# Output projection in five unequal groups of chunks, residual scaled in place

## The chip, the cores and the metric

The kernel runs on one core of a Trainium2 chip. The metric is device time in microseconds of one execution, median over runs. The engines have one instruction queue each and run it in order: TensorE (PE in the profile, its weight loads PEld), VectorE (DVE), ScalarE (ACT), GpSimd (POOL) and SyncE (SP), which here only issues transfers.

## The reference, cut to what matters

One layer on 1024 tokens and 16 meta tokens, width 1024. A normalised input is projected; three mixers (pooling, 256 columns; forgetting attention and stick-breaking attention, 384 columns each) give y of 1024 columns. Then:

```python
h = h + jnp.concatenate([y_pool, y_fox, y_sb], axis=-1) @ w_out[i]
a = rmsnorm(h, norm2[i])
h = h + (jax.nn.silu(a @ w_gate[i]) * (a @ w_up[i])) @ w_down[i]
```

and a final norm. The change concerns the first of these lines and the scaling in the second.

## The kernel before

**Precision.** Every fp32 operand is split into a high part and the rest. A product of two such operands takes three matmuls: high by high, high by rest, rest by high. The split of y and of the weights `w_out` is done on POOL: a copy (`hi_pool`, which the profile gives as L77) and a subtraction (L681 or L674 for weights, L690 for y).

**Output projection.** y lies in eight chunks of 128 columns in memory (`ysd`), and `w_out` in eight chunks of 128 rows. The residual `h` (tile `x1`, in the profile x) has eight token blocks of 128 x 1024, blocks 0 to 3 are half j = 0, blocks 4 to 7 are j = 1. The chunks are summed in four groups of two, `OGROUPS = ((5, 2), (3, 4), (0, 1), (6, 7))`, each for both halves, so in eight passes. `out_load` prepares a pass: weights of the group, if they aren't there, and the y chunks of the half. `out_part` walks its four token blocks, `out_block` does one: for each half of the 1024 columns, 2 x 3 matmuls into one PSUM tile `mm` (two buffers), and an addition of it into `h` on VectorE (L703). That is 8 passes x 4 blocks x 2 = 64 additions.

**Buffers.** Weights of groups 0 and 2 use the four `xa` tiles, those of groups 1 and 3 the four `wa` tiles, two per chunk. A y chunk takes two of eight `xb` tiles; raw data pass through `yr` (three) and `wor` (two). A tile is taken again as soon as its last reader is done.

**What runs beside it.** The attention of six pairs of heads is one stream, everything else (input projections, then the output projection) another, the filler. `interleave` mixes their emission by estimated costs: `GOALS` says how much filler goes beside each pair, `X5` how much beside the last, whose chunk 7 is the last y to come. A scheduler then orders each engine's queue by priority; attention gets a boost of 300. The last pair walks its tiles from large to small (t = 3 to 0, both heads of each), and its `head_norm` makes `last_y[1]` (tiles 3 and 2) and `last_y[0]` (tiles 1 and 0). Its sum passes ScalarE, POOL (tile `pt`; ScalarE for the last), VectorE and two matmuls with `hmean` (L410, L411), then L413 to L415 and the split (L566, L567).

**The last passes.** Group 3, chunks 6 and 7, is done by `out_last`, j = 1 and then j = 0. After a block's additions it squares `h` on ScalarE into a scratch tile `hs` (an `xa` tile), makes the norm's factor `r2`, writes `hs = h * r2`, and stores `h` to memory (`hsd`, SP), where the end of the kernel fetches it. `turn_block` transposes `hs` on PE, `split_block` splits it into `bs`.

**Behind it.** The gated network starts with two chunks done directly (`direct`, L890, chunk pairs with the j = 1 half first, then j = 0), then ten rounds of a Strassen scheme (`strassen`), whose first weight loads stand in SP's queue behind stores of the direct part.

Of the kernel before, what the change touches and what calls it, by code (L numbers as in the profile page):

```python
# [8 lines left out]
F32 = mybir.dt.float32  # L9
F32R = mybir.dt.float32r  # L10
BF16 = mybir.dt.bfloat16
AF = mybir.ActivationFunctionType
# [3 lines left out]
D = 1024  # L16
# [14 lines left out]
def hymba_trunk(  # L31
# [19 lines left out]
    nc = tc.nc  # L51
    V, S, G, PE = nc.vector, nc.scalar, nc.gpsimd, nc.tensor

    def pool(name, side=None, space=None, bufs=1):
        kw = {}
        if side is not None:
            kw["side"] = side
        if space is not None:
            kw["space"] = space
        return tc.tile_pool(name=name, bufs=bufs, reuse_waits="tile", **kw)  # L60
# [3 lines left out]
    def T(p, shape, dt, tag, bufs=1):  # L64
        uid[0] += 1
        return p.tile(list(shape), dt, tag=tag, bufs=bufs, name=f"{tag}_{uid[0]}")
# [3 lines left out]
    PAIRS = [((i >= 3), (2 + i - 3 if i >= 3 else 11 + i), 2 * (i % 3), (2 + i - 3 if i >= 3 else 5 + i))  # L70
             for i in (0, 3, 4, 5, 1, 2)]
# [4 lines left out]
    def hi_pool(o, i):  # L76
        G.tensor_scalar(o, i, 1.0, 0.0, ALU.mult, ALU.add)  # L77
# [9 lines left out]
    x0 = x0_stack.enter_context(pool("x0", side="right"))  # L87
# [3 lines left out]
    def mm(tag, shape, bufs):  # L91
        return T(ps, shape, F32, tag, bufs)
# [272 lines left out]
    def project(pr, c):  # L365
        WPE[0] = G
        w = wload(c + 3)
        new_keys(pr)
        for t0, n in KPIECES:
            o = []  # L370
            yield from proj_piece(w, t0, n, o)
            keys(pr, t0, n, o[0])
        w = wload(c)
        new_queries(pr)
        for j in (1, 0):
            o = []
            yield from proj_piece(w, NM + 512 * j, 512, o)
            queries(pr, j, o[0])
        yield from values(pr, c + 6)
# [283 lines left out]
    def split_weights(g, c):  # L663

        wp, tag = (x0, "xa") if g % 2 == 0 else (regions["wo"], "wa")
        wh = T(wp, [128, D + 32 * (g % 2 == 0)], F32R, tag, 4)[:, :D]
        wl = T(wp, [128, D + 32 * (g % 2 == 0)], F32R, tag, 4)[:, :D]
        if g == 0:
            for q in range(4):
                raw = T(r1, [128, 2, 128], F32, "wr", 4).rearrange("p a b -> p (a b)")  # L670
                qs = slice(256 * q, 256 * q + 256)
                nc.sync.dma_start(raw, w_out[128 * c:128 * c + 128, qs])
                hi_pool(wh[:, qs], raw)
                G.tensor_tensor(wl[:, qs], raw, wh[:, qs], ALU.subtract)  # L674
        else:
            for q in range(2):
                raw = T(regions["wo"], [128, 512], F32, "wor", 2)
                qs = slice(512 * q, 512 * q + 512)
                nc.sync.dma_start(raw, w_out[128 * c:128 * c + 128, qs])
                hi_pool(wh[:, qs], raw)  # L680
                G.tensor_tensor(wl[:, qs], raw, wh[:, qs], ALU.subtract)  # L681
        return wh, wl

    def split_y(c, j):
        raw = T(x0, [128, T0], F32, "xb", 8)[:, :512] if regions["wo"] is None else T(regions["wo"], [128, 512], F32, "yr", 3)
        nc.sync.dma_start(raw, ysd[c][:, 512 * j:512 * j + 512])
        yh = T(x0, [128, T0], F32R, "xb", 8)[:, :512]
        hi_pool(yh, raw)
        yl = T(x0, [128, T0], F32R, "xb", 8)[:, :512]
        G.tensor_tensor(yl, raw, yh, ALU.subtract)  # L690
        return yh, yl

    def out_block(b, tb, yy, ws):
        ts_ = slice(128 * tb, 128 * tb + 128)
        for dh in range(2):
            ds = slice(512 * dh, 512 * dh + 512)
            p = mm("mm", [128, 512], MMB)
            i = 0
            for (yh, yl), (wh, wl) in zip(yy, ws):
                for y_, w_ in ((yh, wh), (yh, wl), (yl, wh)):  # L700
                    PE.matmul(p, y_[:, ts_], w_[:, ds], start=i == 0, stop=i == 3 * len(ws) - 1)  # L701
                    i += 1
            V.tensor_tensor(h[b][:, ds], p, h[b][:, ds], ALU.add)  # L703
            yield 0.65 * len(ws)

    def out_load(g, j):
        if g not in wts:
            wts[g] = [split_weights(g, c) for c in OGROUPS[g]]
        return [last_y[j] if c == PAIRS[5][3] else split_y(c, j) for c in OGROUPS[g]]

    def out_part(g, j, yy=None):

        if yy is None:
            yy = out_load(g, j)
        for tb in range(4):
            yield from out_block(4 * j + tb, tb, yy, wts[g])

    def out_last(j):

        step = out_part(len(OGROUPS) - 1, j, ylast[j])  # L720
        for tb in range(4):
            b = 4 * j + tb
            next(step)
            next(step)
            hs = T(x0, [128, D + 32], F32, "xa", 4)[:, :D]
            S.activation(hs, h[b], AF.Square, accum_out=ssq2[:, b:b + 1])
            if j:
                S.activation(r2[:, b:b + 1], ssq2[:, b:b + 1], AF.Ln, scale=1.0 / D, bias=epst[:, 0:1])
                S.activation(r2[:, b:b + 1], r2[:, b:b + 1], AF.Exp, scale=-0.5)
            else:  # L730
                G.tensor_scalar(r2[:, b:b + 1], ssq2[:, b:b + 1], 1.0 / D, EPS, ALU.mult, ALU.add)
                G.tensor_tensor(r2[:, b:b + 1], r2[:, b:b + 1], mhalf[:, 0:1], ALU.pow)
            S.activation(hs, h[b], AF.Copy, scale=r2[:, b:b + 1])
            nc.sync.dma_start(hsd[b], h[b])
            hss[b] = hs
            yield 1.3

    def turn_block(b):
# [16 lines left out]
    OGROUPS = ((5, 2), (3, 4), (0, 1), (6, 7))  # L755
    wts, bf, bs, hss, last_y = {}, {}, {}, {}, {}
    dpool = ctx.enter_context(tc.tile_pool(name="dp", bufs=1, space=bass.MemoryType.DRAM))
    ysd = {c: dpool.tile([128, SEQ], F32, name=f"ysd{c}") for c in range(8)}
    hsd = [dpool.tile([128, D], F32, name=f"hsd{b}") for b in range(8)]
# [4 lines left out]
    ssq2 = cst.tile([128, 8], F32, name="ssq2")  # L764
    r2 = cst.tile([128, 8], F32, name="r2")
# [37 lines left out]
    def after(g, n, s):  # L803

        for i, c in enumerate(g):
            yield c
            if i == n:
                yield from s

    regions = {"wo": None}  # L810
    h = {}

    def open_out():
        first = out_load(0, 1)
        for b in (4, 5, 6, 7, 0, 1, 2, 3):
            h[b] = T(hp, [128, D], F32, "x1", 8)
            nc.sync.dma_start(h[b], xtok[NM + 128 * b:NM + 128 * b + 128, :])
        r1_stack.close()
        wos.enter_context(x0_stack.pop_all())
        regions["wo"] = wos.enter_context(pool("wo", side="right"))  # L820
        yield from out_part(0, 1, first)

    wos = ExitStack()
    project_first(prs[0], PAIRS[0][1])
# [5 lines left out]
    def filler():  # L830
        for p in range(1, 6):
            gen = project(prs[p], PAIRS[p][1])
            if p == 1:
                gen = after(gen, FGS, forget_gates())
            for ci in range(2):
                if p == POOLS[ci]:
                    yield from pool_pieces(ci)
            yield from gen
        yield from open_out()
        for g, j in ((0, 0), (1, 1), (1, 0), (2, 1), (2, 0)):  # L840
            yield from out_part(g, j)

    SBC, FOXC = 65.0, 38.0
    PC, UC = 32.6, 12.0
    AHEAD, X4, X5, X6 = 12.0, 20.0, 43.0, 12.0
    BOOST = 300
    POOLS = (2, 4)
    GOALS = (PC + 8, PC + 4, PC, PC + UC, PC - AHEAD + X4, X5)
    att, f = Stream(attention(), BOOST), Stream(filler())
    goal = AHEAD  # L850
    for p in range(6):
        goal += GOALS[p]
        interleave(att, FOXC if PAIRS[p][0] else SBC * (0.7 if p == 5 else 1), f, goal - f.at)
    f.finish()
    g = len(OGROUPS) - 1
    ylast = {1: out_load(g, 1)}
    y6 = split_y(OGROUPS[g][0], 0)
    f = Stream(out_last(1))
    interleave(att, SBC * 0.3, f, X6)
    f.finish()  # L860
    ylast[0] = [y6, last_y[0]]
    at_stack.close()
    attn_stack.close()

# [41 lines left out]
    for _ in out_last(0):  # L906
        pass
# [105 lines left out]
    for c0 in range(2, FF, 2):  # L1013
# [6 lines left out]
        for key, x in up.items():  # L1020
            g = gate[key]
# [34 lines left out]
    h = {}  # L1056
# [123 lines left out]
```

## Time and profile before

| what | value |
|---|---|
| three runs, median | 1284.89 us (1284.74 to 1286.3) |
| profiled execution | 1286.02 us, span 1284.2 us |
| granted TensorE clock, mean | 0.982 |
| PE busy, share of span | 1215.3 us, 95% |
| DVE busy | 947.2 us, 74% |
| ACT busy | 630.5 us, 49% |
| POOL busy | 480.2 us, 37% |
| L701, first and last start | 474.8 and 633.9 us |
| L703, 64 additions, median | 681 ns |

The span is from the first to the last instruction; the 1.8 us beside it lie around them. Matmuls are pipelined, so that a row of several has a duration longer than the distance of their starts; a pace is read from the starts. In rows of a timeline the columns are start, duration, engine, line, operation, output and inputs, shapes, count, and in brackets the engine's idle time before it and who ended it.

### The profile page before, as it was taken

What the parts mean: (1) busy time and instruction counts of PE and PEld (TensorE: products, weight loads), DVE (VectorE), ACT (ScalarE), POOL (GpSimd) and SP (SyncE); (2) the same over time, 40 slices, a digit from 0 to 9 for tenths busy, and PEclk for the clock granted to TensorE, in tenths of its full rate; (3) what the DMA queues carried; (4) which work ended last, traced back from release to release, by engine and by line L of the source; (5) the groups of instructions that cost most, each with busy time, mean ns of one, the idle gap of its engine ahead of it and who ended that gap; (6) DMA issues with size and microseconds to landing.
All of it is one profiled execution on the core that took longest, in us unless ns stands there. A gap on an engine that the chain in (4) does not pass through costs nothing.

```text
span 1284.2 us, 18471 instructions
## 1 busy us (share of the span) xinstructions
PE 1215.3 (95%) x6310; PEld 1023.5 (80%) x6310; DVE 947.2 (74%) x1713; ACT 630.5 (49%) x1318; POOL 480.2 (37%) x534
## 2 busy tenths in 40 slices
PE   7699899999898989999898999999999999999997
PEld 5587778888788878778687888888888888788885
DVE  8667886868977779997777676666767656876557
ACT  6456754645448677767743333332223334444443
POOL 6459046362363764550105453443544410000001
PEclk9999899999899989999999999999999999999999
DMA  5100011010100161201505554445544439565653
GB/s 180 40 17 27 13 47 34 26 42 18 50 29 30 38 213 67 74 25 50 197 25 180 171 167 151 138 136 181 189 164 160 136 131 344 172 212 199 197 173 139
DMA packets 73146, 147.13 MB, mean 115 GB/s; under 512 B 9052, under 2 KB 21340, under 8 KB 73052
## 3 DMA queue, kind: packets, MB, share of 16 engines
q1 hardware_dynamic: 69728, 142.01, 33.3%
q10 hardware_dynamic: 3324, 3.95, 0.9%
q8 instruction: 50, 0.82, 0.3%
q14 instruction: 44, 0.36, 0.1%
HBM read 103.98 MB, written 41.94 MB: 114 GB/s over the span
## 4 chain that ended last, share of the span: by engine, by line
PE 66%; DVE 11%; issue 4%; ACT 4%; DMA 2%; POOL 1%; SPq 0%; DVEq 0%; POOLq 0%; ACTq 0%
PE s L890 21%; PE mm L289 10%; PE mm L890 8%; PE s L1075 7%; PE mm L701 4%; PE o L511 4%; PE mm L1075 3%; PE o L1075 3%; PE s L531 3%; DVE r L470 3%; PE s L429 1%; PE s L431 1%; DVE x L703 1%; DVE P L472 1%; DMA raw<-in_w_down 1%
## 5 line engine op out<-in xcount | busy, mean ns | idle before, releaser
L890 PE MATMUL s<-t,wh 128*128 128x512 f32 x544 | 170.4, 392 | 3.5 <-ACT wh L876 3.5
L890 PEld LDWEIGHTS s<-t,wh 128*128 128x128 f32 x544 | 102.7, 189 | 25.7 <-ACT wh L876 4.2
L890 PE MATMUL s<-s,wh 128*128 128x512 f32 x384 | 118.5, 390 | 0.0
L876 ACT CAST wh<-ss 128x512 fp32r<-128x512 f32 x80 | 49.5, 621 | 133.6 <-PE s L890 93.0
L890 PE MATMUL s<-t,wl 128*128 128x512 f32 x272 | 106.3, 391 | 0.0
L289 PE MATMUL mm<-x,wh 128*128 128x512 f32 (+1 forms) x320 | 100.1, 387 | 1.1 <-DVE pt L354 1.1
L538 ACT CAST ph<-s 128x512 fp32r<-128x512 f32 (+2 forms) x168 | 70.7, 434 | 60.0 <-PE s L531 23.9
L890 PE MATMUL mm<-t,wh 128*128 128x512 f32 x320 | 98.5, 389 | 0.0
L1063 ACT CAST wh<-sg 128x512 fp32r<-128x512 f32 x74 | 46.0, 623 | 104.6 <-PE s L1075 46.1
L876 ACT CAST wh<-raw 128x512 fp32r<-128x512 f32 x68 | 41.7, 621 | 111.2 <-PE s L890 72.4
L539 DVE TENSOR_TENSOR pl<-s,ph 128x512 fp32r<-128x512 f32 (+2 forms) x168 | 81.1, 492 | 19.9 <-ACT ph L538 17.5
L1064 DVE TENSOR_TENSOR wl<-sg,wh 128x512 fp32r<-128x512 f32 x74 | 51.0, 690 | 56.9 <-ACT wh L1063 56.6
L511 PE MATMUL o<-pl,v 128*128 128x256 f32 (+1 forms) x288 | 85.8, 314 | 0.7 <-DVE pl L521 0.6
L511 PE MATMUL o<-ph,v 128*128 128x256 f32 (+1 forms) x288 | 80.2, 292 | 3.8 <-ACT ph L520 2.4
L890 PEld LDWEIGHTS s<-s,wh 128*128 128x128 f32 x384 | 71.9, 188 | 14.9
L984 DVE TENSOR_TENSOR cg<-s,tmp 128x512 f32<-128x512 f32 x60 | 41.2, 687 | 56.9 <-PE s L890 56.9
L1114 POOL TENSOR_TENSOR r<-r,mhalf 128x1 f32<-128x1 f32 x8 | 4.4, 547 | 209.0 <-DVE r L1113 207.4
L289 PE MATMUL mm<-xa,wh 128*128 128x264 f32 (+3 forms) x248 | 78.5, 320 | 1.2 <-ACT rbc L239 0.7
L289 PE MATMUL mm<-xa,wl 128*128 128x264 f32 (+3 forms) x248 | 76.5, 313 | 1.2 <-POOL wl L164 1.2
L289 PE MATMUL mm<-xb,wh 128*128 128x264 f32 (+3 forms) x248 | 77.0, 313 | 0.0
L531 PE MATMUL s<-ident,P 128*128 128x128 f32 x432 | 68.8, 278 | 6.3 <-DVE pl L521 3.6
L878 DVE TENSOR_TENSOR wl<-ss,wh 128x512 fp32r<-128x512 f32 x80 | 68.7, 862 | 8.2 <-ACT wh L876 6.8
(287 smaller groups left out, 3636.6 us busy)
## 6 DMA issues: line engine op xcount, KB each, us to landing
sg<-lsd SPq DMA_DIRECT2D x70, 256.0 KB, 3.2
raw<-in_w_gate SPq DMA_DIRECT2D x22, 512.0 KB, 5.4
raw<-in_w_up SPq DMA_DIRECT2D x22, 512.0 KB, 3.9
wr<-in_w_in SPq DMA_DIRECT2D x80, 128.0 KB, 2.2
raw<-in_w_down SPq DMA_DIRECT2D x20, 512.0 KB, 3.6
lsd<-cg SPq DMA_DIRECT2D x40, 256.0 KB, 3.2
raw<-rsd SPq DMA_DIRECT2D x40, 256.0 KB, 3.4
raw<-in_w_down SPq DMA_DIRECT2D x34, 256.0 KB, 3.1
```

Source lines behind the costliest of these rows:

```text
L289: PE.matmul(p[:, :n], w[k][ww], xx(k, t0, n), start=i == 0, stop=i == 23)
L511: PE.matmul(po[:, c:256], pr.v[h][:, kb, :], x, start=first and ix == 0, stop=(kb == nkb - 1 and ix == 1), skip_group_check=True)
L531: PE.transpose(tp[:, gi, ii, :], ptiles[ii][:, kc], ident)
L538: S.copy(ph[:, a:b], tpf[:, a:b])
L539: V.tensor_tensor(pl[:, a:b], tpf[:, a:b], ph[:, a:b], ALU.subtract)
L701: PE.matmul(p, y_[:, ts_], w_[:, ds], start=i == 0, stop=i == 3 * len(ws) - 1)
L876: S.copy(wh, a)
L878: V.tensor_tensor(wl, a, wh, ALU.subtract)
L890: PE.matmul(p, ws[ww][:, k, :], xs_[xx][:, k, :], start=first and i == 0, stop=i == 11, skip_group_check=True)
L1063: S.copy(wh, a)
L1064: V.tensor_tensor(wl, a, wh, ALU.subtract)
L1075: PE.matmul(p, x[xx][:, 128 * b:128 * b + 128], y[yy], start=first and i == 0, stop=last and i == 2, skip_group_check=True)
```

## The change

The chunks are summed in five passes: group 0 for j = 1; groups 0 and 1 for j = 0; groups 1 and 2 for j = 1; group 3 for j = 1; groups 2 and 3 for j = 0. A pass of two groups sums 4 x 3 matmuls in one PSUM tile, so there are 5 x 4 x 2 = 40 additions; the matmuls are the same 384. The weights of groups 2 and 3, four chunks, are resident in `xa` and `wa` during the last pass. The y chunks of that pass are prepared ahead of the j = 1 pass of group 3. As `xa` is then taken, `h` is scaled in place; the square's result goes, in bf16, into a `wor` tile, and the store of `h` stands ahead of the square, since the scaling overwrites what it reads. `X5` goes from 43 to 32.

```diff
-    def out_load(g, j):
-        if g not in wts:
-            wts[g] = [split_weights(g, c) for c in OGROUPS[g]]
-        return [last_y[j] if c == PAIRS[5][3] else split_y(c, j) for c in OGROUPS[g]]
+    def out_load(gs, j):
+
+        for g in gs:
+            if g not in wts:
+                wts[g] = [split_weights(g, c) for c in OGROUPS[g]]
+        return [last_y[j] if c == PAIRS[5][3] else split_y(c, j) for g in gs for c in OGROUPS[g]]
...
-            yield from out_block(4 * j + tb, tb, yy, wts[g])
+            yield from out_block(4 * j + tb, tb, yy, [w for g in gs for w in wts[g]])
...
-            hs = T(x0, [128, D + 32], F32, "xa", 4)[:, :D]
-            S.activation(hs, h[b], AF.Square, accum_out=ssq2[:, b:b + 1])
+            nc.sync.dma_start(hsd[b], h[b])
+            sq = T(regions["wo"], [128, D], BF16, "wor", 2)
+            S.activation(sq, h[b], AF.Square, accum_out=ssq2[:, b:b + 1])
...
-            S.activation(hs, h[b], AF.Copy, scale=r2[:, b:b + 1])
-            nc.sync.dma_start(hsd[b], h[b])
-            hss[b] = hs
+            S.activation(h[b], h[b], AF.Copy, scale=r2[:, b:b + 1])
+            hss[b] = h[b]
...
-        for g, j in ((0, 0), (1, 1), (1, 0), (2, 1), (2, 0)):
-            yield from out_part(g, j)
+        yield from out_part((0, 1), 0)
+        yield from out_part((1, 2), 1)
...
-    AHEAD, X4, X5, X6 = 12.0, 20.0, 43.0, 12.0
+    AHEAD, X4, X5, X6 = 12.0, 20.0, 32.0, 12.0
...
-    ylast = {1: out_load(g, 1)}
-    y6 = split_y(OGROUPS[g][0], 0)
+
+    ylast = {1: ((3,), 1, out_load((3,), 1))}
+    y01 = out_load((2,), 0)
+    y6 = split_y(OGROUPS[3][0], 0)
...
-    ylast[0] = [y6, last_y[0]]
+    ylast[0] = ((2, 3), 0, y01 + [y6, last_y[0]])
```

The queues show three places. First POOL's, before the change, at the end of the last pair's attention: the second half of chunk 7's weights, then chunk 6 of y for both halves (`yr_7711`, `yr_7717`), then the head norm's copy `pt` and the copy of `last_y[1]`.

```order
L681 TENSOR_TENSOR wa_7702<-wor_7703,wa_7701 128x512
L77 TENSOR_SCALAR wa_7701<-wor_7707 128x512
L681 TENSOR_TENSOR wa_7702<-wor_7707,wa_7701 128x512
L77 TENSOR_SCALAR xb_7713<-yr_7711 128x512
L690 TENSOR_TENSOR xb_7715<-yr_7711,xb_7713 128x512
L77 TENSOR_SCALAR xb_7719<-yr_7717 128x512
L690 TENSOR_TENSOR xb_7721<-yr_7717,xb_7719 128x512
L77 TENSOR_SCALAR pt_7620<-nt_7618 128x512
L77 TENSOR_SCALAR q_1871_7631<-nt_7617 128x512
```

The same place of POOL's queue now; `yr_7609`, `yr_7615` and `yr_7621` are chunks 0, 1 and 6 of j = 0.

```order
L77 TENSOR_SCALAR xb_7611<-yr_7609 128x512
L77 TENSOR_SCALAR wa_7593<-wor_7595 128x512
L690 TENSOR_TENSOR xb_7613<-yr_7609,xb_7611 128x512
L77 TENSOR_SCALAR wa_7593<-wor_7599 128x512
L77 TENSOR_SCALAR xb_7617<-yr_7615 128x512
L681 TENSOR_TENSOR wa_7594<-wor_7595,wa_7593 128x512
L681 TENSOR_TENSOR wa_7594<-wor_7599,wa_7593 128x512
L690 TENSOR_TENSOR xb_7619<-yr_7615,xb_7617 128x512
L77 TENSOR_SCALAR xb_7623<-yr_7621 128x512
L77 TENSOR_SCALAR pt_7512<-nt_7510 128x512
L690 TENSOR_TENSOR xb_7625<-yr_7621,xb_7623 128x512
L77 TENSOR_SCALAR q_1844_7523<-nt_7509 128x512
```

Two more chunks of y stand ahead of `pt`, and all of these rows, with those of chunk 6's weights ahead of them, now come behind the pass (1, 2), whose tiles they take.

Second, ScalarE's queue before, where block 6 (`x_1552_6375`) and block 7 (`x_1553_6377`) are scaled and `last_y[0]` is normalised (L413, L414, L566):

```order
L733 ACTIVATE xa_7837<-x_1552_6375,r_556 128x1024
L413 ACTIVATE nt_8009<-o_8006,epst 128x512
L726 ACTIVATE xa_7922,ssq_555<-x_1553_6377 128x1024
L414 ACTIVATE nt_8009<-nt_8009 128x512
L728 ACTIVATE r_556<-ssq_555,epst 128x1
L729 ACTIVATE r_556<-r_556 128x1
L733 ACTIVATE xa_7922<-x_1553_6377,r_556 128x1024
L566 CAST xb_8013<-nt_7999 128x512
```

And now:

```order
L736 ACTIVATE x_1552_6375<-x_1552_6375,r_556 128x1024
L413 ACTIVATE nt_7913<-o_7910,epst 128x512
L729 ACTIVATE wor_7827,ssq_555<-x_1553_6377 128x1024
L414 ACTIVATE nt_7913<-nt_7913 128x512
L731 ACTIVATE r_556<-ssq_555,epst 128x1
L732 ACTIVATE r_556<-r_556 128x1
L736 ACTIVATE x_1553_6377<-x_1553_6377,r_556 128x1024
L566 CAST xb_7917<-nt_7903 128x512
```

The order is the same, but L736 writes the tile that the store of `h` reads, so it waits for that store, and L566 stands behind it.

Third, PE's queue behind the transposes of the last block (L744, `xa_8223`) before; the products `s_8386` belong to the direct part with j = 1 (inputs `s_`), and 12 of them stand here ahead of the first one with j = 0 (inputs `t_`):

```order
L744 MATMUL o_8267<-ident,xa_8223 128x128 x4
L744 MATMUL o_8273<-ident,xa_8223 128x128 x4
L890 MATMUL s_8386<-s_8035,wh_8137 128x512
L890 MATMUL s_8386<-s_8036,wh_8137 128x512
L890 MATMUL s_8386<-s_8035,wl_8139 128x512
```

The same place now (lines are three higher, `x_1557_6385` is the block):

```order
L746 MATMUL o_8219<-ident,x_1557_6385 128x128 x4
L746 MATMUL o_8225<-ident,x_1557_6385 128x128 x4
L893 MATMUL s_8311<-s_7939,wh_8031 128x512
L893 MATMUL s_8311<-s_7940,wh_8031 128x512
L893 MATMUL s_8311<-s_7939,wl_8033 128x512
L893 MATMUL s_8338<-s_7936,wh_8037 128x512
L893 MATMUL s_8338<-s_7937,wh_8037 128x512
```

These transposes now stand further ahead among the direct products: 27 of them with j = 1 follow here, the last three of `s_8311` and all 24 of `s_8338`, before the first one with j = 0.

More of the change, by code (lines that the diff above doesn't have):

```diff
@@ L704, in out_block, with out_part @@
             yield 0.65 * len(ws)
-    def out_load(g, j):
-        if g not in wts:
-            wts[g] = [split_weights(g, c) for c in OGROUPS[g]]
-        return [last_y[j] if c == PAIRS[5][3] else split_y(c, j) for c in OGROUPS[g]]
-    def out_part(g, j, yy=None):
+    def out_load(gs, j):
[3 more added lines that the diff above has]
+        return [last_y[j] if c == PAIRS[5][3] else split_y(c, j) for g in gs for c in OGROUPS[g]]
+    def out_part(gs, j, yy=None):
         if yy is None:
-            yy = out_load(g, j)
+            yy = out_load(gs, j)
         for tb in range(4):
-            yield from out_block(4 * j + tb, tb, yy, wts[g])
+            yield from out_block(4 * j + tb, tb, yy, [w for g in gs for w in wts[g]])
     def out_last(j):
-        step = out_part(len(OGROUPS) - 1, j, ylast[j])
+        step = out_part(*ylast[j])
         for tb in range(4):
@@ L813, in open_out @@
     def open_out():
-        first = out_load(0, 1)
+        first = out_load((0,), 1)
         for b in (4, 5, 6, 7, 0, 1, 2, 3):
@@ L820, in open_out @@
         regions["wo"] = wos.enter_context(pool("wo", side="right"))
-        yield from out_part(0, 1, first)
+        yield from out_part((0,), 1, first)
     wos = ExitStack()
@@ L854, in hymba_trunk @@
     f.finish()
-    g = len(OGROUPS) - 1
-    ylast = {1: out_load(g, 1)}
-    y6 = split_y(OGROUPS[g][0], 0)
+    ylast = {1: ((3,), 1, out_load((3,), 1))}
+    y01 = out_load((2,), 0)
+    y6 = split_y(OGROUPS[3][0], 0)
     f = Stream(out_last(1))
```

## The prediction

> **What bounds the kernel now.** I read the page first, then busy time by stretches, then the waits of the stage that the change touches.
>
> ```profile
> span 1284.2 us, 18471 instructions
> PE 66%; DVE 11%; issue 4%; ACT 4%; DMA 2%; POOL 1%; SPq 0%; DVEq 0%; POOLq 0%; ACTq 0%
> ```
>
> TensorE (PE) carries two thirds of the chain that ended last. The output projection (L701) runs from 475 to 634 us, partly beside the last pair's attention. These stretches show that stage (us, then busy time of each engine, granted clock, DMA):
>
> ```profile
> core 0: us, PE busy (x) PEld busy (x) DVE busy (x) ACT busy (x) POOL busy (x), PEclk, DMA share, GB/s
> 518.00:536.00 18.00, 15.86 (x86) 12.47 (x85) 17.29 (x28) 11.59 (x26) 14.41 (x13) 1.00 0.37 116
> 536.00:556.00 20.00, 19.54 (x108) 16.12 (x106) 18.14 (x31) 14.69 (x34) 4.50 (x6) 1.00 0.05 15
> 556.00:571.00 15.00, 13.83 (x77) 11.42 (x78) 13.75 (x24) 8.83 (x21) 9.98 (x10) 1.00 0.16 53
> 571.00:586.00 15.00, 14.02 (x78) 11.50 (x78) 14.31 (x28) 9.93 (x28) 2.80 (x3) 1.00 0.00 1
> 597.00:617.00 20.00, 17.75 (x97) 14.21 (x95) 14.39 (x27) 17.62 (x35) 0.00 (x0) 1.00 0.27 106
> 678.00:690.00 12.00, 8.60 (x31) 6.74 (x32) 8.62 (x8) 5.62 (x10) 9.82 (x7) 0.86 0.36 122
> ```
>
> From 518 to 586 VectorE (DVE) is busy 63.5 of 68 us and PE 63.3: both are near their limit. Who waits for whom between 497 and 623 us (total, times, longest):
>
> ```profile
> POOL wa L77 <- PE mm L701: 15.5, 1, 15.5
> POOL xa L77 <- PE mm L701: 14.6, 1, 14.6
> PE mm L701 <- DVE x L703: 6.6, 10, 1.5
> ```
>
> PE's idle time in the stage is mostly the wait for an addition (L703) to free one of two PSUM buffers. POOL, which prepares weights and y, waits 15 us for PE and is never waited for.
>
> **A: fewer additions beside the attention.** VectorE's costliest groups between 500 and 579 us, from the first scores of the last pair to those before its last tiles:
>
> ```profile
> L703 DVE TENSOR_TENSOR x<-mm,x 128x512 f32<-128x512 f32 x34 | 23.0, 676 | 1.3 <-PE mm L701 1.3
> 597.63 1.28 DVE L703 TENSOR_TENSOR x<-mm,x 128x512 f32<-128x512 f32 x2
> ```
>
> A second addition follows after 0.60 us (1.28 less 0.68). VectorE's order now has 16 additions in this stretch: 17 or 18 fewer, 17 x 0.60 = 10.2 us, an upper bound of the gain. Two things use it up. First, one pass now holds four chunks, all eight xb tiles, so the next pass's y and two chunks of weights start only in the last block of the pass. POOL does such work at this pace (twelve rows, the first, one inside and the last):
>
> ```profile
> 551.63 0.62 POOL L77 TENSOR_SCALAR wa<-wor 128x512 fp32r<-128x512 f32 x1 [15.50 <-PE mm L701]
> ...
> 557.00 1.93 POOL L681 TENSOR_TENSOR wa<-wor,wa 128x512 fp32r<-128x512 f32 x1
> ...
> 563.47 1.29 POOL L681 TENSOR_TENSOR wa<-wor,wa 128x512 fp32r<-128x512 f32 x1
> ```
>
> Six pairs of copy and subtraction in 13.1 us: 2.19 us a pair. Pass (1, 2) needs four y chunks and four halves of weights, 8 pairs, 17.5 us, before its first blocks close. Attention goes on meanwhile: from 518 to 556 VectorE was busy 35.4 us, 16 additions (9.6 us) among them, and four fifths of that stretch's attention steps stand beside this work in VectorE's new order: 0.8 x 25.8 = about 21 us, so the 17.5 just fit, with little to spare. Second, PE's order puts 24 more projection matmuls ahead of the second head's largest tile. Their pace:
>
> ```profile
> 503.04 2.99 PE L701 MATMUL mm<-xa,xb 128*128 128x512 f32 x12
> 505.88 0.32 PE L429 MATMUL s<-k,q 128*128 128x348 f32 x1
> 520.99 1.66 PE L701 MATMUL mm<-wa,xb 128*128 128x512 f32 x6 [1.49 <-DVE x L703]
> ```
>
> Twelve in 2.84 us, 0.237 us each: 5.7 us, of which waits like the 1.49 there take up some 3. I take half of the bound, **A = -5 us** (from -10 to +1).
>
> **B: the last y of tokens 512 to 1023.** POOL's order now has its head norm's copy (pt) behind both chunks of weights, y6, y0 and y1. Before:
>
> ```profile
> 588.79 0.62 POOL L77 TENSOR_SCALAR pt<-nt 128x512 fp32r<-128x512 f32 x1 [14.90 <-ACT nt L404]
> 570.68 0.28 PE L431 MATMUL s<-k,q 128*128 128x264 f32 x1
> 589.85 0.48 PE L410 MATMUL o<-pt,hmean 128*128 128x512 f32 x1
> ```
>
> From those scores to L410 passed 19.2 us. Now the pass's last block follows the scores, frees tiles after three matmuls (0.7), then POOL does 7 pairs and a copy, 7 x 2.19 + 0.6 = 15.9, then pt: 0.2 + 0.7 + 15.9 + 0.7 = 17.5 us. **B = -1.5** (-3.5 at the 1.92 us of an undisturbed pair, +4.5 at 3.1). Without that queue six fewer additions would have given 3.6. PE waits there: transposes and projection stand behind L410.
>
> **C: more projection behind the attention.** Chunks 0 and 1 of tokens 0 to 511, 48 matmuls, now come after it: 48 x 0.237 = +11.4 us of PE work. Part fills waits:
>
> ```profile
> 613.79 1.09 PE L744 MATMUL s<-ident,xa 128*128 128x128 f32 x8 [1.66 <-ACT xa L733]
> 617.71 3.06 PE L701 MATMUL mm<-wa,xb 128*128 128x512 f32 x12 [0.55 <-DVE x L703]
> 621.91 1.66 PE L701 MATMUL mm<-wa,xb 128*128 128x512 f32 x6 [1.14 <-DVE x L703]
> ```
>
> These waits are 3.35 us; with 0.2 us of restart at each and the smaller stalls up to 650 us, about 5.5. The first blocks of the new pass run while the last y is normalised, so I leave 1.5 of it: **C = +11.4 - 4 = +7.4**.
>
> The scaling in place must now wait until its store to memory (hsd) has landed. Square and scale on ScalarE, and landings of blocks 4 to 7, then 0 to 3:
>
> ```profile
> L726 ACT ACTIVATE xa<-x x8: 1043/1057/1059, 598.9 to 636.3; 128x1024 f32<-128x1024 f32 x8
> DMA to landing us min/median/max: 2.6/2.6/3.0
> DMA to landing us min/median/max: 2.8/4.7/6.6
> ```
>
> For blocks 4 to 7, 2.6 us stand against 1.06 + 0.19 + 0.5 of square, read-out and r: ScalarE is held about 1 us more per block. Queued behind it are the next block's square and L413 and L566, which make the last y; PE has 18 new matmuls (4.3 us) and 24 transposes to cover that. For blocks 0 to 3 an addition of 0.9, a landing of 6.6 and a scale of 1.15 end 9 us after the block, and PE's order has at least 43 matmuls (9.9 us) between a block and its transposes. I count the store at nothing beyond the 1.5 above; without this cover it costs up to 6.6 - 1.8 = 4.8 us once.
>
> **D: the bubble before the Strassen part.** Behind the last block's transposes:
>
> ```profile
> 650.01 1.29 DVE L745 TENSOR_TENSOR f<-o,n 128x512 f32<-128x512 f32 x2 [4.37 <-PE o L744]
> 673.24 0.68 DVE L1038 TENSOR_TENSOR sg<-raw 128x512 f32<-128x512 f32 x1
> 678.09 1.26 POOL L989 TENSOR_TENSOR ss<-raw 128x512 f32<-128x512 f32 x1 [39.73 <-DMA raw<-in_w_gate]
> 677.47 0.39 PE L890 MATMUL mm<-t,wl 128*128 128x512 f32 x1
> 681.40 1.58 PE L890 MATMUL s<-t,wh 128*128 128x512 f32 x4 [3.54 <-ACT wh L876]
> 685.67 0.63 PE L890 MATMUL s<-t,wh 128*128 128x512 f32 x2
> 686.59 0.62 PE L890 MATMUL s<-t,wh 128*128 128x512 f32 x2
> ```
>
> VectorE has no pause between the first two rows; behind the second SP issues a load, POOL and ScalarE follow, and PE waits 3.54 us. From 681.40 ten matmuls take 4.27 us instead of 2.3 (four take 0.92 from 685.67): 2.0 us more. PE's order now has 27 matmuls of the direct product behind those transposes, not 12; 15 x 0.23 = 3.45 us more work cover the same VectorE chain. The wait shrinks to 0.1 to 0.5 us and the slow stretch goes: **D = -5.2** (0 if the transposes come late).
>
> [...]
>
> **E: slow clock in B.** In 571 to 586 some 40 of PE's 78 matmuls were projection, 9.5 of its 14.0 us; attention alone left 4.5 in 15 us. In B's 17.5 us that is 5.3, with 13 projection matmuls 8.4: PE idles about 9 us, in pieces. A like place, behind pauses of at most 0.72 us:
>
> ```profile
> 474.84 2.77 PE L701 MATMUL mm<-xa,xb 128*128 128x512 f32 x6
> 479.31 1.55 PE L701 MATMUL mm<-xa,xb 128*128 128x512 f32 x6
> ```
>
> Six matmuls cost 1.2 us more. Bounds 0 and 2.0 (the bubble); I take **E = +1**.
>
> **Sum**: -5 - 1.5 + 7.4 - 5.2 + 1 = -3.3 us. The profiled execution took 1286.02, 1.8 more than its span; it would take 1282.7. It stands 1.1 above the median of the three runs, 1284.89; for a median I say **1281.6**.
>
> **Rivals.** *POOL becomes the bound* (slower). 15 pairs of A and B lie on the path; at 2.7 us a pair, between the mean and the 3.1 of disturbed ones, 15 x 0.51 less 0.9 of slack = 6.8 us more: 1288.4. It decides from 2.6 us a pair. For it: the 1.93 against 1.29 above, beside a busy VectorE. Against it: VectorE has less to do. [...] No wait of before shows POOL late.
> *The bubble stays* (no change): the store of block 3 is late behind weight loads in SP's queue, so D = 0 and the time is 1286.8. For it: landings of 6.6 us. Against it: the 9.9 us of matmuls.
> *The relief does not arrive* (no change): attention hangs on its own ScalarE and VectorE steps, A = -1: 1285.6. Against it: VectorE's 94% in A's stretch.
> *The relief arrives whole*: A = -9, 1277.6.
> That additions are not saved is excluded: the order has 40 for 64.
>
> **How the numbers follow.** Forecast 0.38, whole relief 0.14, bubble 0.15, no relief 0.13, POOL 0.20. About 0.2%, 2.6 us, can be told from no change: below 1282.3 faster, above 1287.5 slower. Hence 0.52, 0.28, 0.20. The range of 1276 to 1288.5 takes in A's bound without its last us and POOL at 2.7.
>
> **What would show it.** A: about 16 additions between the first scores of the last pair and its last tiles, and these some 5 us earlier. B: L410's pt waits for POOL, not for L404. C: few gaps between the last y and the last projection block. D: no gap over 1 us at the Strassen start, and a granted clock near 1.00 there. I am wrong if PE waits on xb or wa for several us inside the attention, or if ScalarE's scaling holds up the last y.

## The result, and the profile after

| | before | with the change |
|---|---|---|
| median of 20 runs each | 1285.8 us (1284.06 to 1288.51) | 1288.9 us (1285.43 to 1291.34) |
| ratio to before, 95% interval | | 1.002 (1.0012 to 1.0027) |
| profiled execution, span | 1286.02 us, 1284.2 us | 1285.43 us, 1283.6 us |

The change makes the kernel 0.2% slower (0.08% in a second set of runs, whose interval takes in no change); -3.3 us had been forecast. The profile on the right is of the quickest of its 20 runs, and it reaches the first projection matmul 1.6 us sooner than the profile before (473.2 against 474.8), in code that both share. So the spans of these two profiles say nothing, and I compare the stage that changed, from that matmul to the twelfth of the Strassen part, in four stretches:

| stretch, by PE | before: us, projection matmuls | after: us, projection matmuls | difference less 0.237 us for each matmul moved |
|---|---|---|---|
| S1: first L701 to the scores of t = 1, second head | 95.84, 240 | 92.87, 228 | -0.1 |
| S2: to L410 of `last_y[1]` | 19.17, 51 | 19.54, 18 | +8.2 |
| S3: to the last L701 | 44.07, 93 | 52.05, 138 | -2.7 |
| S4: to the twelfth Strassen matmul | 51.75 | 47.42 | -4.3 |
| sum | 210.83 | 211.88 | +1.05 |

The last column takes out the projection matmuls that merely come earlier or later, and leaves mostly PE's idle and slow time. It does not take out nine transposes of the attention (L517, L531) that stood in S3 and now stand in S2 (33 there instead of 24), about 1 us at 0.11 us each. The first two stretches, before and then after (us, busy time of PE, PEld, VectorE, ScalarE and POOL, granted clock, DMA):

```profile
474.84:570.68 95.84, 91.28 (x495) 75.02 (x495) 88.77 (x150) 67.69 (x159) 50.72 (x48) 0.99 0.22 73
570.68:589.85 19.17, 18.19 (x103) 14.88 (x103) 18.26 (x36) 13.85 (x39) 3.74 (x4) 1.00 0.00 1
```

```profile
473.21:566.08 92.87, 88.59 (x484) 72.83 (x483) 80.16 (x133) 67.55 (x160) 36.46 (x34) 0.99 0.21 68
566.08:585.62 19.54, 13.80 (x80) 10.82 (x79) 18.11 (x33) 13.66 (x40) 18.00 (x17) 0.89 0.14 41
```

PE's idle time (stretch less busy) hardly changed in S1, 4.6 and 4.3 us. It rose in S2 from 1.0 to 5.7 us and fell in S3 from 4.0 to 2.1 and in S4 from 3.5 to 1.3, so that its sum is 13.1 us before and 13.4 after. The rest of the 1.05 us is pace: half clock for 6.8 us in S2 and S3, which had none before, against 3.4 us in S4, which now has none.

The stage is far steadier than the whole: a second profile of before gives 210.79, three more of the change 211.98, 212.57 and 212.91. So the stage is 1.1 to 2.1 us longer, and the medians differ by 1.9 to 3.1; where the rest lies the profiles do not show.

The chain of the page after (shares of the span by engine) is PE's more than before:

```profile
span 1283.6 us, 18446 instructions
PE 74%; DVE 10%; ACT 3%; issue 1%; POOL 0%; DMA 0%; ACTq 0%; DVEq 0%; POOLq 0%
```

Busy time by stretches after, at places 1.6 us earlier than those of the first four rows of the prediction's table, then the 8 us behind them and the Strassen start:

```profile
core 0: us, PE busy (x) PEld busy (x) DVE busy (x) ACT busy (x) POOL busy (x), PEclk, DMA share, GB/s
516.40:534.40 18.00, 16.88 (x91) 13.60 (x90) 16.57 (x25) 13.44 (x31) 12.46 (x13) 1.00 0.23 67
534.40:554.40 20.00, 16.84 (x93) 13.04 (x92) 19.25 (x31) 14.09 (x33) 6.88 (x5) 1.00 0.19 60
554.40:569.40 15.00, 14.77 (x81) 12.02 (x79) 10.73 (x20) 10.07 (x25) 1.98 (x2) 1.00 0.00 1
569.40:584.40 15.00, 9.50 (x61) 7.37 (x60) 13.90 (x26) 11.05 (x33) 15.00 (x16) 0.90 0.18 54
584.40:592.40 8.00, 7.36 (x41) 6.61 (x40) 5.21 (x13) 4.74 (x14) 1.64 (x2) 0.75 0.00 0
...
679.00:691.00 12.00, 10.75 (x48) 8.44 (x47) 8.83 (x9) 5.70 (x11) 9.32 (x7) 1.00 0.33 101
```

In the third row it is VectorE that has time to spare, in the fourth PE: from 554 VectorE, relieved of additions, is busy 10.7 of 15 us where it was 13.75, and then PE is busy 9.5 of 15 us where it was 14.02. The granted clock falls to 0.90 and 0.75 there and no longer at the Strassen start.

VectorE's additions (L703) from 498 to 577 us after, and who waits for whom in the stage:

```profile
L703 DVE TENSOR_TENSOR x<-mm,x 128x512 f32<-128x512 f32 x16 | 10.5, 678 | 0.8 <-PE mm L701 0.8
```

```profile
POOL wa L77 <- PE mm L701: 26.1, 1, 26.1
...
DVE pl L539 <- ACT ph L538: 5.3, 8, 1.2
...
DVE e L469 <- ACT e L467: 3.7, 3, 1.9
PE mm L701 <- DVE x L703: 3.5, 5, 1.5
PE s L531 <- DVE P L472: 3.3, 3, 1.5
...
PE s L531 <- DVE pl L539: 2.1, 2, 1.2
```

16 additions, as counted from the order, and PE's waits for an addition fell from 6.6 to 3.5 us. In their place PE waits for the attention's own results, P (L472) and pl (L539), and VectorE for ScalarE. POOL still waits 26 us for PE.

PE's rows from the scores at the end of S1 to the first matmul with `last_y[1]` (q):

```profile
566.08 0.28 PE L431 MATMUL s<-k,q 128*128 128x264 f32 x1
...
572.51 0.73 PE L701 MATMUL mm<-wa,xb 128*128 128x512 f32 x2 [1.45 <-DVE x L703]
...
575.80 0.71 PE L701 MATMUL mm<-wa,xb 128*128 128x512 f32 x2
...
578.39 0.41 PE L517 MATMUL s<-ident,P 128*128 128x128 f32 x2 [0.44 <-DVE P L472]
579.97 1.00 PE L531 MATMUL s<-ident,P 128*128 128x128 f32 x7 [1.16 <-DVE P L472]
581.90 0.69 PE L517 MATMUL s<-ident,P 128*128 128x128 f32 x2 [0.93 <-DVE P L472]
583.79 1.75 PE L531 MATMUL s<-ident,P 128*128 128x128 f32 x7 [1.19 <-DVE pl L539]
...
585.62 0.77 PE L410 MATMUL o<-pt,hmean 128*128 128x512 f32 x1
...
591.68 1.19 PE L701 MATMUL mm<-wa,q 128*128 128x512 f32 x4 [0.49 <-POOL q L77]
```

The last projection matmuls that don't need q are issued at 575.8; for 15.3 us PE has only the attention, and stands four times for it. The pair of transposes at 578.39 takes 0.41 us, that at 581.90 takes 0.69: half clock, from 581.5 until about 588.3.

### The profile page after: what moved, and what is told of

It reads as the page before. It is cut to its first block, busy times and chain, and to the rows that moved or that the text cites. A ratio compares the mean times of both kernels' runs of the same rounds, so it can differ in the third digit from the quotient of the medians.

```text
span 1283.6 us, 18446 instructions
## 1 busy us (share of the span) xinstructions
PE 1214.2 (95%) x6310; PEld 1022.9 (80%) x6310; DVE 936.3 (73%) x1689; ACT 629.9 (49%) x1318; POOL 479.5 (37%) x534
## 4 chain that ended last, share of the span: by engine, by line
PE 74%; DVE 10%; ACT 3%; issue 1%; POOL 0%; DMA 0%; ACTq 0%; DVEq 0%; POOLq 0%
PE s L893 24%; PE mm L289 10%; PE s L1078 9%; PE mm L893 8%; PE mm L701 6%; PE o L511 4%; PE mm L1078 3%; PE o L1078 3%; PE s L531 3%; DVE r L470 2%; PE s L429 1%; PE s L431 1%; DVE P L472 1%; ACT e L461 1%; DVE P L495 1%
## 5 line engine op out<-in xcount | busy, mean ns | idle before, releaser
L539 DVE TENSOR_TENSOR pl<-s,ph 128x512 fp32r<-128x512 f32 (+2 forms) x168 | 81.1, 493 | 24.3 <-ACT ph L538 22.0
L531 PE MATMUL s<-ident,P 128*128 128x128 f32 x432 | 70.1, 281 | 12.5 <-DVE P L472 4.8
L1078 PE MATMUL s<-wl,wh 128*128 128x512 f32 x192 | 74.7, 389 | 0.0
```

Of the source, the lines that this page charges most:

```text
L531: PE.transpose(tp[:, gi, ii, :], ptiles[ii][:, kc], ident)
L539: V.tensor_tensor(pl[:, a:b], tpf[:, a:b], ph[:, a:b], ALU.subtract)
L1078: PE.matmul(p, x[xx][:, 128 * b:128 * b + 128], y[yy], start=first and i == 0, stop=last and i == 2, skip_group_check=True)
```

## Experiments

Ratios are to the kernel before, run beside each kernel on the same chip, with 95% intervals. Medians of different rows can come from different chips, on which the kernel before took 1285.6 to 1287.0 us, so rows are best compared by ratio. The first row has 20 runs, split_late 5, keep_warm 4, the others 11 or 12. S1 and S2 are differences from before as in the last column above, in us; "rest" runs from L410 to a matmul 112 us behind the twelfth of the Strassen part (the 2100th from the end), which every version has.

| kernel | additions | median us | ratio (interval) | S1 | S2 | rest |
|---|---|---|---|---|---|---|
| change (first profile) | 40 | 1288.9 | 1.002 (1.0012 to 1.0027) | -0.1 | +8.2 | -6.7 |
| change again | 40 | 1288.89 | 1.0008 (0.9995 to 1.0021) | -0.3 | +8.2 | -6.3 |
| adds_back | 64 | 1292.71 | 1.0036 (1.0024 to 1.0048) | -0.1 | +3.1 | +3.0 |
| late_half | 56 | 1289.84 | 1.0018 (1.0006 to 1.0031) | +0.6 | +6.8 | -2.8 |
| early_half | 48 | 1286.61 | 0.9992 (0.998 to 1.0004) | +1.1 | +3.6 | -2.7 |
| split_early | 56 | 1283.87 | 0.9985 (0.9972 to 0.9999) | +0.4 | +3.1 | -6.0 |
| split_early2 (the same) | 56 | 1284.48 | 0.9987 (0.9976 to 0.9999) | +0.7 | +3.1 | -5.9 |
| split_late | 48 | 1296.97 | 1.008 (1.0068 to 1.0092) | +0.2 | +8.2 | +2.1 |
| split_first | 48 | 1285.04 | 0.9987 (0.9974 to 0.9999) | -0.4 | +5.0 | -6.6 |
| split_second | 48 | 1286.09 | 1.0001 (0.9992 to 1.001) | 0.0 | +7.1 | -6.3 |
| tail_cover | 40 | 1288.63 | 1.0018 (1.0008 to 1.0028) | +3.8 | +6.1 | -7.7 |
| inplace_only | 64 | 1285.34 | 0.9997 (0.9988 to 1.0006) | 0.0 | 0.0 | -0.2 |
| keep_warm | 40 | 1297.24 | 1.0085 (1.0072 to 1.0099) | -0.1 | +10.8, 3.8 of it added work | -2.8, with 2.8 of added work |

**The change once more** (no edit).

> The changed kernel unaltered, for a second profile. Its first profile is of 1285.43 us, the lowest of 20 runs with a median of 1288.9, and counted from the first projection matmul it is only about 1 us longer than before. Theory P (pauses of the attention): the missing 2 to 3 us lie between 500 and 600 us, where PE waits for the softmax (L472) and the granted clock falls: a profile of some 1288 to 1290 us shows a clock under 0.83 in 580 to 600 us, or a second slow stretch near 535. Rival S (scatter): they lie outside this stretch, in code that both kernels share, and the stretch from the first projection matmul to the Strassen part is the same within 1 us as in the first profile.

This profile too lies under the median, at 1286.33 us, with the same 6.8 us of half clock between 580 and 590 and 211.98 us in the stage. It shows that the first profile was no accident in the stage, and doesn't show where the slower runs lose their time.

**All additions back, the rest of the change kept.**

```diff
-            p = mm("mm", [128, 512], MMB)
...
+            for g in range(0, len(ws), 2):
+                p = mm("mm", [128, 512], MMB)
...
+                    PE.matmul(p, y_[:, ts_], w_[:, ds], start=i == 0, stop=i == 5)
...
+                V.tensor_tensor(h[b][:, ds], p, h[b][:, ds], ALU.add)
```

> The changed kernel with one PSUM tile and one addition per group again: 64 additions, 24 of them back in passes (0,1) j=0, (1,2) j=1 and (2,3) j=0; passes, weights, y and the in-place scaling as in the change. If fewer additions relieve VectorE at 0.60 us each where 16 of them went beside the attention, this is 5 to 10 us slower than the change (1294 to 1299 us). Theory P (the attention hangs on its own steps, the relief is not used): within 2 us of the change.

Slower, by 3.8 us against the change run beside it, which lies between the two forecasts, and yet not for the reason that the relief theory gives: S2 is 5 us better with the additions than without. The loss is all behind the attention, where the version has PE's order with the direct matmuls ahead of the last transposes. The Strassen start of this kernel, as PE's row:

```profile
688.43 2.07 PE L894 MATMUL s<-t,wh 128*128 128x512 f32 x4 [3.19 <-ACT wh L880]
```

The gap of before is back, 3.19 us, with four matmuls at half pace behind it (2.07 us for four). The verdict of the whole kernel alone would have been read the wrong way.

**The halves of the change.** Late: passes of two chunks beside the attention, four only in the last.

```diff
-        yield from out_part((0, 1), 0)
-        yield from out_part((1, 2), 1)
+        for g, j in ((0, 0), (1, 1), (1, 0), (2, 1)):
+            yield from out_part((g,), j)
```

> Only the late half of the change: passes (0) j=1, (0) j=0, (1) j=1, (1) j=0, (2) j=1 with two chunks each as before, then (3) j=1 and (2,3) j=0 as in the change, with the in-place scaling; 56 additions. Theory P: the loss lies in the four-chunk passes beside the attention and the gain of some 7 us behind it, so this is 3 to 6 us faster than before (1280 to 1283). Rival L (the loss comes with work moved behind the attention: 24 matmuls fewer beside it leave it without cover): 1285 to 1289. If POOL's queue ahead of pt is what costs, it is no better than the change either, since y0, y1 and y6 stand there too.

Early: (2) j=0 again beside the attention, group 3 alone behind it, scaling into a tile of its own.

```diff
         yield from out_part((1, 2), 1)
+        yield from out_part((2,), 0)
...
-    ylast[0] = ((2, 3), 0, y01 + [y6, last_y[0]])
+    ylast[0] = ((3,), 0, [y6, last_y[0]])
```

> Only the early half: passes (0) j=1, (0,1) j=0, (1,2) j=1, (2) j=0, then (3) j=1 and (3) j=0 as before, with the scaling into a tile of its own; X5 43 as before; 48 additions. Theory P: the four-chunk passes gain nothing beside the attention and starve it of cover, but (2) j=0 is again there to fill the last tiles: 1285 to 1290, with waits for L472 near the start of pass (1,2). If fewer additions are a relief: 1278 to 1282, as 14 additions less stand beside the attention and nothing is moved behind it. The wait of 3.5 us before the Strassen part is back in both.

The first miss of my theory, which had put the whole loss on the four-chunk passes. The late half is no faster but slower than before: 48 projection matmuls fewer (not the 24 of the expectation) are issued before the attention's last one, 270 for 318, and S2 has 6.8 us more of idle and slow time, more than the 2.8 us won behind. The early half stays level. Its profile (1289.4 us) was the slowest of its 12 runs, so its stretches show a bad case.

**Two chunks per addition beside the attention, four in the last pass; and the reverse.** In `out_block`, split_early first, then split_late:

```diff
+            m = 4 if len(ws) == 4 and yy[3] is last_y.get(0) else 2
+            for g in range(0, len(ws), m):
...
```

```diff
+            m = 4 if len(ws) == 4 and yy[3] is not last_y.get(0) else 2
+            for g in range(0, len(ws), m):
...
```

> The change with one addition per group (two chunks) again in the passes beside the attention, (0,1) j=0 and (1,2) j=1, and one for four chunks kept in the last pass, (2,3) j=0: 56 additions. PE's order behind the attention is that of the change. Theory H (a four-chunk block holds PE's in-order queue and its PSUM tile until the fourth chunk of y is there, and puts its matmuls in large lumps, which costs more than the additions it saves): 3 to 4 us faster than the change, 1284 to 1286. Theory R (fewer additions are a relief beside the attention): 3 to 6 us slower than the change, 1292 to 1295.

> The reverse: four chunks per addition beside the attention as in the change, and two in the last pass, (2,3) j=0: 48 additions. PE's order up to the end of the attention is that of the change; behind it direct matmuls are drawn ahead of the last transposes, so that fewer stand behind them. Theory H with step D of the prediction: the 3.5 us bubble before the Strassen part and its slow clock are back, and waits for the last split at 650 to 660: 5 to 8 us slower than the change, 1294 to 1297. If the direct matmuls behind the transposes don't decide the bubble: 1289.

Both as theory H had it. That fewer additions are a relief on balance is excluded: 16 more of them beside the attention make the kernel 3 to 4.5 us faster than the change, by the ratios. split_early is also faster than the kernel before, in two sets of 12 runs whose intervals both lie under 1. split_late has the change's S1 and S2 and loses 8.8 us of rest, with the gap again, though here the clock stayed at 1.00 behind it. Its row:

```profile
690.32 1.26 PE L895 MATMUL s<-t,wh 128*128 128x512 f32 x4 [3.26 <-ACT wh L881]
```

> The version with additions of two chunks beside the attention and of four in the last pass, once more, for its time: it was 0.15% faster than the kernel before, with an interval that nearly reaches 1. If that is real: a ratio of 0.997 to 0.9995 again.

late_half and split_early have the same 56 additions, two chunks each beside the attention, and the same last pass; they differ only in how the passes beside the attention are grouped, (0) j=0, (1) j=1, (1) j=0, (2) j=1 against (0, 1) j=0, (1, 2) j=1. By the ratios split_early is 0.3% faster. So the passes of four chunks are not what costs beside the attention; the sums of four chunks in one PSUM tile are, with the order that the scheduler makes of them.

**Idle matmuls in the pauses.** Four of 128 x 512 ahead of the transposes of the last pair's last tiles; they add work and leave none out.

```diff
+    def warm(pr, h, t, tp):
+        if pr is prs[5] and (t == 0 or t == 1 and h == 1):
+            for _ in range(4):
+                PE.matmul(tp, pr.q1[h][0][:, 0:128], pr.k1[h][:, 0:512], start=True, stop=True, skip_group_check=True)
```

> The change with 28 idle matmuls of 128x512 (0.237 us each, 6.6 us in all) put ahead of the last pair's transposes of tiles t = 1 (second head) and t = 0, each into the tile that the transposes overwrite: PE has something to do in the pauses between 570 and 590. Theory P (slow clock): the granted clock of 580 to 600 is 1.00 instead of 0.83, some 3.4 us less lost there, while about half of the 6.6 us falls into pauses: 1287 to 1290, so no slower than the change in spite of 6.6 us more work. If the pauses and not the clock are what costs: 1292 to 1295.

A failed experiment, above both forecasts. PE's rows of this kernel (L509 are the idle matmuls) show why:

```profile
581.61 1.00 PE L538 MATMUL s<-ident,P 128*128 128x128 f32 x7 [1.16 <-DVE P L472]
583.55 2.08 PE L509 MATMUL s<-k,q 128*128 128x512 f32 x4 [0.93 <-DVE P L472]
585.42 0.63 PE L523 MATMUL s<-ident,P 128*128 128x128 f32 x2
```

The tile into which they write is itself free only when VectorE has read it for P, so the first of them stood behind the same pause instead of filling it, and all four ran at half clock. 16 of the 28 stand in S2, the others behind it. Half clock lasts 3.4 us instead of 6.8 (0.91 for 0.83 in 580 to 600), but 6.6 us of work for that is no bargain, and pauses and clock are not told apart by it.

**The scaling in place alone**, on the kernel before.

```diff
-            hs = T(x0, [128, D + 32], F32, "xa", 4)[:, :D]
-            S.activation(hs, h[b], AF.Square, accum_out=ssq2[:, b:b + 1])
+            nc.sync.dma_start(hsd[b], h[b])
+            sq = T(regions["wo"], [128, D], BF16, "wor", 2)
+            S.activation(sq, h[b], AF.Square, accum_out=ssq2[:, b:b + 1])
```

> The kernel before with nothing but the scaling in place: store, square into bf16, scale of the residual itself, which waits for the store to land. Prediction's step C: hidden, 1284.5 to 1287.5, as before. If ScalarE, held by the landing of blocks 4 to 7 (2.6 us against 1.75), delays the last y: 1 to 5 us more than before.

Level with before, and within 0.2 us of it in every stretch of the table. The wait for the store exists (in the change, L736 waits for hsd):

```profile
  DMA hsd<-x: 5.4, 3
```

5.4 us of ScalarE in three waits. inplace_only has three such waits too, 4.7 us in all, and loses nothing by them.

**Further profiles of the change, and one of before** (no edits).

> The changed kernel, one more profile. Both profiles so far (1285.43 and 1286.33 us) lie 2.5 to 3.5 us under its median, with two stretches of half clock at 580 to 590. Theory C: the time of single executions differs by the number of such stretches of some 3.4 us: one of 1288 us or more has one or two more of them, in places where PE pauses, and its idle time without them is the same. Rival: the clock is as in the first two, and the idle time itself is longer.

> The changed kernel once more, with the same two answers: more stretches of half clock at the same idle time (theory C), or the same clock (0.982) and more idle time (rival).

> The kernel before, a second profile, to see which of the places of half clock in its first one are there again. Theory C: at 460 and behind the 3.5 us gap before the Strassen part always, elsewhere now and then, none between 560 and 600 us, where the projection covers the attention's pauses.

They took 1292.48, 1287.45 and 1286.77 us. Stretches of after_p3, then of after_p4, then of before_p2:

```profile
520.00:545.00 25.00, 21.14 (x113) 16.30 (x112) 23.40 (x35) 18.48 (x42) 18.41 (x17) 1.00 0.25 81
1080.00:1120.00 40.00, 37.45 (x158) 30.34 (x157) 29.35 (x47) 18.76 (x31) 0.00 (x0) 0.96 0.68 226
```

```profile
520.00:545.00 25.00, 20.99 (x106) 16.32 (x105) 23.04 (x35) 17.00 (x37) 20.03 (x17) 0.93 0.26 86
1080.00:1120.00 40.00, 38.26 (x169) 31.38 (x168) 32.30 (x51) 20.08 (x34) 0.00 (x0) 1.00 0.66 219
```

```profile
520.00:545.00 25.00, 22.82 (x125) 18.27 (x124) 24.29 (x40) 16.11 (x35) 13.32 (x12) 1.00 0.28 88
1080.00:1120.00 40.00, 38.35 (x169) 31.46 (x168) 32.60 (x53) 19.64 (x33) 0.00 (x0) 1.00 0.66 215
```

Theory C holds for part of it. All four profiles of the change have 6.8 us of half clock that begin between 581 and 586 us; neither profile of before has any between 500 and 680, and both have it at the Strassen start. after_p3 has a stretch of half clock near 1100, in code that both kernels share, and it came to the stage 3.3 us later than the mean of the three other profiles of the change (477.0 against 473.7), in such code too: scatter that is not the change's. after_p4 has one of its own near 540, behind PE's longest wait for POOL in any profile of the change:

```profile
541.37 1.22 PE L701 MATMUL mm<-xa,xb 128*128 128x512 f32 x2 [1.80 <-POOL xb L690]
```

Among the runs whose clock is on record, 104 of the kernel before took 1286.48 us on average at a granted clock of 0.98194, 34 of the change 1288.61 at 0.98021. Take off all that the clock can have held back, (1 - clock) x 1286 us, and 1263.25 and 1263.15 are left, so the clock is enough to make the whole difference. That it makes the whole is not shown: among runs of one kernel the time rises by only 0.43 us (before) and 0.68 us (change) for each 0.001 less of clock, not by 1.29, and by these slopes 0.7 to 1.2 of the 2.1 us are the clock's. The gain of split_early over the change is not one of clock: its two sets have 0.9802 and 0.9794.

**What it is in the four-chunk sums.** Two chunks per addition in one of the two passes only: split_first in (0,1) j=0, split_second in (1,2) j=1.

```diff
+            m = 2 if b < 4 and yy[-1] is not last_y.get(0) else len(ws)
```

```diff
+            m = 2 if b >= 4 else len(ws)
```

> Two chunks per addition in pass (0,1) j=0 alone, four in (1,2) j=1 and in (2,3) j=0: 48 additions. PE's order has its projection here in larger lumps than the change, one of 23 matmuls (5.5 us) without a step of the attention. Theory H in its form of lumps: no better than the change, 1288 to 1291. If what counts is the number of matmuls that a PSUM tile must collect before it closes (12 or 6): half of the gain of the split, some 1286 to 1287.

> The reverse: two chunks per addition in pass (1,2) j=1 alone, 48 additions; lumps of at most 12 matmuls. Theory H in its form of lumps: between the change and the version with both passes split, 1285 to 1288. By the size of the PSUM sums: half of the gain too, 1286 to 1287.

The lumps fall: split_first, with its run of 23 projection matmuls, has the ratio of split_early2 (0.9987), and split_second, whose runs are at most 12 long, gains less (1.0001). But half of the gain for each, as the size of the sums would have it, is not what came either: split_first has nearly the whole gain of the split. So the sums of four chunks cost in the pass (0, 1) j=0 above all, and what is special there is not shown.

**More work out of the attention.**

```diff
-        yield from out_part((1, 2), 1)
+        yield from out_part((1,), 1)
...
-    ylast = {1: ((3,), 1, out_load((3,), 1))}
+    ylast = {1: ((2, 3), 1, out_load((2, 3), 1))}
```

> Another 24 matmuls taken out of the attention: passes (0) j=1, (0,1) j=0, (1) j=1 beside it, then (2,3) j=1 and (2,3) j=0; 40 additions as in the change. PE's order then has 83 matmuls of the attention without a projection between, for 33 in the change. If work moved out of the attention is paid there as idle time and only partly returned behind it, this is 3 to 8 us slower than the change (1292 to 1297), with more stretches of half clock. If 5.7 us more of work behind the attention covers the waits there for free: 1286 to 1289.

Level with the change (1.0018), so the loss does not simply grow with the work moved. PE is bare of projection for all of S2, with the lowest clock of any profile there,

```profile
560.00:580.00 20.00, 14.65 (x72) 12.61 (x71) 16.30 (x35) 18.26 (x54) 0.62 (x1) 0.68 0.00 0
```

but its S2 lasts only 13.2 us. Beside 18 projection matmuls the change takes 19.5, beside 30 split_early 17.3.

## Why the prediction was wrong

**A, the step that failed.** It took half of 17 x 0.60 us, VectorE's own time for the additions, as gain, because VectorE was busy 94% of the time. What PE could win by fewer additions in S1 was its wait for them there, 3.7 us, and other waits took their place. PE's waits in S1, before and then after:

```profile
PE mm L701 <- DVE x L703: 3.7, 5, 1.5
```

```profile
PE s L531 <- DVE P L472: 2.2, 2, 1.5
PE s L531 <- DVE pl L539: 0.9, 1, 0.9
PE mm L701 <- DVE x L703: 0.6, 2, 0.3
```

The measured S1 is 3.0 us shorter, but 12 projection matmuls of it (2.8 us) only come later: the relief is 0.1 us. VectorE's freed time went into its own waits for ScalarE (in S1 3.9 us for pl and 3.7 for e, where it had been 1.4 and 1.8), and PE stood for P and pl. That a nearly full engine is the bound was an inference from a share of busy time; by these waits the chain there runs around PE, ScalarE and VectorE in turn. The rival "the relief does not arrive" was right about this (it had 0.13), and split_early shows that additions there are even cheap: 16 more of them, and 3 to 4.5 us less. Why sums of four chunks cost PE time is shown only in its size, not settled. One thing is seen: with sums of two chunks PE has 30 instead of 18 projection matmuls left for S2, to lay over its pauses; split_first gains 3 us there with 18, so this is not all.

**B, right in POOL, wrong in PE.** POOL's row for pt after:

```profile
583.53 0.61 POOL L77 TENSOR_SCALAR pt<-nt 128x512 fp32r<-128x512 f32 x1
```

It begins 17.45 us after the scores of 566.08; the step's chain had it near 17. (Its own 17.5 less 19.2 is -1.7, not -1.5.) But L410 followed at 19.54 instead of 17.5, since PE itself had not got there: four waits for P and pl, and half clock. So +0.4 instead of -1.5. The rival "POOL becomes the bound" falls as a cause of the typical loss: PE waits for POOL 0.5 us for q and some tenths for xb. Single runs come near it (1.80 us in after_p4).

**E, mis-sized, outside its own bounds.** 9 us of PE idling in pieces was foreseen, and 5.7 came; the price was put at 1 us, at most 2.0. Half clock lasts 6.8 us there, by the rows at 569.40 and 584.40 0.10 x 15 + 0.25 x 8 = 3.5 us lost at most, since PE stood for part of it. No gap of PE there is longer than 1.45 us, so the clock fell there without one long gap like the 3.54 us that before has ahead of the Strassen part; why it falls behind short pauses no run here shows.

**C, right.** +8.0 instead of +7.4 (44.07 to 52.05 us), with 45 instead of 48 matmuls moved. Of the 2.7 us in the table only 1.9 are idle time that went, not 4; the rest is mostly the nine transposes that S2 took over. A new wait for an addition (1.22 us at 614.28) took some of the gain. The store was counted as nothing, and inplace_only agrees.

**D, right, a little too large.** The gap and its slow clock:

```profile
682.40 1.24 PE L893 MATMUL s<-t,wh 128*128 128x512 f32 x4 [1.25 <-ACT wh L879]
...
685.09 0.62 PE L893 MATMUL s<-t,wh 128*128 128x512 f32 x2
```

3.54 became 1.25 and the half clock went: -4.3 instead of -5.2, the wait being longer than the 0.1 to 0.5 foreseen. (From 681.40 to 685.67 before stand eleven matmuls, not the ten of the prediction, so the slow stretch was worth some 1.7 us and not 2.0.) adds_back and split_late, which put direct matmuls back ahead of the last transposes, bring gaps of 3.2 and 3.3 us back.

By elapsed time S1 to S4 give -3.0 + 0.4 + 8.0 - 4.3 = +1.1 us in the first profile, up to +2.1 in the others, against -3.3: A missed by 2.0, B and E together by 0.9, C by 0.6, D by 0.9. That A's miss looks small is the moved work: what S1 was shorter by was owed, and S2, in which 33 more matmuls are missing (7.8 us), was not shorter at all.

## What to carry to other kernels

An engine at 94% that stands in a ring with others need not be the bound (VectorE was busy 8.6 us less in S1, and the relief was 0.1 us): before counting a relief, find a row in which the others wait for it and nothing else is late. Work that fills another stage's pauses can be paid where it is taken away (33 matmuls, 7.8 us, left S2, which took 19.54 us instead of 19.17); count elapsed time with the moved work taken out, stretch by stretch, since a whole time can rise for a reason at another place (adds_back). The useful form of this change is split_early: its five passes and its last pass with sums of four chunks, the additions beside the attention kept at two: 0.13 to 0.15% faster than before.

## What was unexpected of the hardware

The clock halved without a long gap: in the 3.4 us before 581.5 us PE ran nine transposes, busy 1.41 us, with no pause over 1.2 us, and was then at half clock for 6.8 us:

```profile
578.10:581.50 3.40, 1.41 (x9) 0.93 (x9) 3.34 (x7) 3.35 (x12) 3.40 (x4) 1.00 0.02 5
581.50:588.30 6.80, 5.20 (x23) 4.69 (x23) 4.66 (x10) 2.62 (x9) 3.92 (x4) 0.50 0.00 0
```

The length of a pause alone does not decide; in these traces its place counts too. In the first profiles of before and of the change the stretches of half clock each begin on one grid of 3.41 us: in the change's at 458.6, 472.3 and 581.5 us, which are 4 and 32 steps apart, in that of before at 460.3, 473.9 and 682.1 us, 4 and 61 steps apart. Near 1100 a pause of 1.96 us in early_half lay whole within one step, and the clock halved behind it:

```profile
1098.50:1101.90 3.40, 1.44 (x7) 0.88 (x6) 3.40 (x7) 0.62 (x1) 0.00 (x0) 1.00 0.10 28
1101.90:1105.30 3.40, 3.40 (x10) 2.63 (x9) 2.84 (x5) 1.23 (x2) 0.00 (x0) 0.50 0.85 283
```

In split_late the pause of 3.26 us ahead of the Strassen part fell into two steps, 1.64 and 1.62 us, and the clock stayed whole, while in adds_back one of 3.19 us at the same place had 2.4 us in one step and halved it. These are split_late's two steps:

```profile
685.30:688.70 3.40, 1.76 (x8) 1.13 (x6) 0.27 (x1) 0.58 (x1) 1.60 (x2) 1.00 0.84 334
688.70:692.10 3.40, 1.78 (x7) 1.16 (x8) 1.80 (x3) 2.36 (x5) 2.15 (x2) 1.00 0.00 0
```

How busy PE must be in a step is not settled: a step with 1.66 us busy kept the clock (after_p4, from 1097.8 us), and so did one with 1.60 us (before, from 43.84 us), while behind one with 2.11 us it halved (before, from 470.51 us).
